# Merge gates of attentions 2 and 3 as seven products of quarters, with sums of tokens made on the chip

## The chip, the cores and the metric

The kernel runs on one core of a Trainium2 chip. The metric is the time on the device of one execution, in microseconds (us). Three runs of the kernel before took 1600.72, 1601.18 and 1605.92 us. One further execution was taken with the profiler. TensorE (PE in the rows) does matrix products, VectorE (DVE), ScalarE (ACT) and GpSimd (POOL) work on elements, SyncE (SP) issues most transfers.

## The reference

An encoder of two layers, 512 tokens of width 1024. In each layer four attentions of different kinds read projections of the normalised input `h`, and their outputs are merged:

```
h = rmsnorm(x);  p = h @ w_in[l]                 # 13824 columns: q, k, v, gate, merge
merged = 0
for n, o in enumerate((oa, ob, oc, od)):         # four attention outputs, 512 wide
    gated = o * silu(p.gate[n])                  # 512 columns
    y = gated @ w_branch[l, n]                   # 512 -> 1024
    merged += sigmoid(p.merge[n]) * y            # 1024 columns
x = x + merged @ w_out[l]                        # 1024 -> 1024
```

The product that the change touches is `p.merge[n] = h @ w_in[l][:, merge n]`, 512 x 1024 by 1024 x 1024, for n = 2 and 3.

## The kernel before

All matrix products run in float16 with operands split into a high and a low half: each product of two values takes three matmuls (high by high, low by high, high by low). `hT_h` and `hT_l` hold the halves of `h`, features on the partitions, 512 tokens along the row.

Weights come from HBM in pieces of 1 MB as float32, in the order of the table `ORDER`. `dma_w` issues the two loads of a piece, `load_w` converts each half piece (128 x 1024) on ACT into `whi` and on DVE into the remainder `wlo`, and `take_w` hands a piece out and starts the next: conversion runs two pieces ahead, loading three. Staging tiles `wst` have five buffers.

`merge(n)` goes feature tile by feature tile (8 of 128 features): `proj_t` makes the gate's 128 x 512 from 8 slices of `h` with 24 matmuls of 512 columns, ACT makes the sigmoid in three passes (Exp, Ln, Exp), `proj_t` makes the branch's 128 x 512 with 12 matmuls, and DVE multiplies the two and adds them to `acc`. The four merges are spread: `weave` runs the steps of an attention with steps of other work between them, and merge(0), (1), (2) are such filling for attentions B, C and D0; merge(3) runs alone behind D0.

`output` makes `merged @ w_out` in seven products of quarters in place of eight (a Winograd form of Strassen's scheme). Operands are cut in halves along both sides, the seven products run on quarters and on sums of quarters, and the results are combined by adding in PSUM and on DVE. The weights' sums are made while loading: a tile `wsum` takes a quarter by an ordinary load, and POOL issues DMAs that add another quarter to it (`accum_op`). One running sum serves four of the seven products: the first use, then three adds, each of which must wait until the sum before has been converted. The token side's sums (`xs`, two kinds for each of four row groups, in `forms`) are made on DVE and ACT, three of the four while merge(3) still runs. In the program's count the products are named by their form, in the order 1, 2, 5, 6, 7, 3, 4; 1, 2 and 4 read a quarter as it is, 5, 6, 7 and 3 read `xs`.

Each engine runs its instructions in its own order, fixed when the program is built: a scheduler with a model of the times reorders the instructions within what dependences allow.

## Time and profile before

| | |
|---|---|
| median of three runs | 1601.18 us |
| profiled execution | 1608.34 us, of which the span from the first to the last instruction is 1606.6 us |
| granted TensorE clock, mean | 0.997 of full |
| busy TensorE / DVE / ACT / POOL | 1588.5 / 1109.9 / 975.7 / 61.0 us |

An engine's busy time is the time in which at least one of its instructions runs; weight loads of TensorE are counted apart (PEld). Matmuls overlap in the rows (a matmul of 512 columns lasts 0.38 us and the next starts 0.22 us later), so the distance between two starts is what one costs. On DVE and ACT too a row's duration holds an overlap of some 0.1 us with its neighbours.

### The profile page before, as it was taken

How to read it: one execution, taken by the hardware profiler on the slowest of the kernel's cores; microseconds unless marked ns; L12 is line 12 of the kernel's file. 1: busy time of each engine (PE TensorE's matmuls, PEld its weight loads, DVE VectorE, ACT ScalarE, POOL GpSimd, SP SyncE). 2: the span in 40 equal slices, each digit the busy share in tenths (PEclk: the TensorE clock that was granted, in tenths of full speed). 3: DMA queues.
4: the chain of work that ended last, by engine and by line, in shares of the span. 5: the costliest groups of instructions: out<-in, count | busy, mean ns of one | idle time of the engine just before them, and what ended most of it. 6: DMA issues, size and time to landing. Idle time of an engine off the chain costs nothing.

```text
span 1606.6 us, 26657 instructions
## 1 busy us (share of the span) xinstructions
PE 1588.5 (99%) x10222; PEld 834.0 (52%) x10222; DVE 1109.9 (69%) x2188; ACT 975.7 (61%) x1799; POOL 61.0 (4%) x145
## 2 busy tenths in 40 slices
PE   8899999999999999999999999999999999999998
PEld 3555455644555554554455545556455655445444
DVE  7599667854757675775877876687556675658565
ACT  7387755765746464654567766566666465556452
POOL 4000000000000000120000000000000000001000
PEclk9999999999999999999999999999999999999999
DMA  9758333522556666465455672335334675743644
GB/s 295 183 150 159 114 97 105 139 79 86 138 139 168 152 196 161 124 188 131 122 189 142 141 156 91 97 97 120 118 99 112 157 184 130 207 131 108 176 92 105
DMA packets 223729, 224.18 MB, mean 140 GB/s; under 512 B 167080, under 2 KB 179384, under 8 KB 223600
## 3 DMA queue, kind: packets, MB, share of 16 engines
q1 hardware_dynamic: 220000, 209.37, 49.1%
q0 software_dynamic: 3600, 13.10, 4.0%
q8 instruction: 80, 1.31, 0.3%
q14 instruction: 49, 0.40, 0.1%
HBM read 172.33 MB, written 10.24 MB: 114 GB/s over the span
## 4 chain that ended last, share of the span: by engine, by line
PE 89%; DMA 3%; DVE 3%; issue 3%; POOL 1%; ACT 1%; POOLq 0%; DVEq 0%; ACTq 0%
PE mm L475 15%; PE mm L473 15%; PE mm L474 15%; PE mm L491 10%; PE mm L492 10%; PE mm L493 10%; PE s L647 3%; PE s L648 3%; PE pv L653 2%; PE pv L654 2%; PE pv L652 2%; DVE wlo L180 1%; DMA wsum<-in_wf_dram 1%; DMA gb<-in_qk_gain_dram 1%; DMA rope_t<-in_rope_dram 0%
## 5 line engine op out<-in xcount | busy, mean ns | idle before, releaser
L473 PE MATMUL mm<-whi,hT_h 128*128 128x512 f16 (+1 forms) x1280 | 473.4, 370 | 8.5 <-DVE qn L543 3.0
L475 PE MATMUL mm<-whi,hT_l 128*128 128x512 f16 (+1 forms) x1280 | 473.5, 370 | 0.6 <-DVE hT_l L289 0.6
L474 PE MATMUL mm<-wlo,hT_h 128*128 128x512 f16 (+1 forms) x1280 | 473.3, 370 | 0.3 <-DVE wlo L180 0.3
L180 DVE SCALAR_TENSOR_TENSOR wlo<-wst,whi 128x1024 f16<-128x1024 f32 (+1 forms) x256 | 300.3, 1206 | 116.8 <-ACT whi L179 116.2
L179 ACT ACTIVATE whi<-wst 128x1024 f16<-128x1024 f32 (+1 forms) x256 | 252.4, 1034 | 134.0 <-PE mm L492 112.1
L473 PEld LDWEIGHTS <-hT_h 128*128 128x128 f16 x1280 | 131.8, 103 | 132.5 <-DVE v L583 4.1
L475 PEld LDWEIGHTS <-hT_l 128*128 128x128 f16 x1280 | 131.7, 103 | 130.9 <-DVE hT_l L289 1.5
L474 PEld LDWEIGHTS <-hT_h 128*128 128x128 f16 x1280 | 131.8, 103 | 130.3 <-issue 6.6
L493 PE MATMUL mm<-hT_h,wlo 128*128 128x512 f16 x512 | 194.0, 379 | 0.0
L492 PE MATMUL mm<-hT_l,whi 128*128 128x512 f16 x512 | 194.0, 379 | 0.0
L491 PE MATMUL mm<-hT_h,whi 128*128 128x512 f16 x512 | 194.0, 379 | 0.0
L638 ACT ACTIVATE t<-t,nm 128x512 f32<-128x512 f32 (+2 forms) x224 | 131.6, 601 | 90.2 <-DVE t L802 36.2
L643 DVE TENSOR_TENSOR pl<-t,ph 128x512 f16<-128x512 f32 (+2 forms) x224 | 118.1, 543 | 32.0 <-ACT ph L642 31.0
L493 PEld LDWEIGHTS <-wlo 128*128 128x128 f16 x768 | 75.1, 98 | 88.1
L491 PEld LDWEIGHTS <-whi 128*128 128x128 f16 x768 | 75.1, 98 | 86.3
L492 PEld LDWEIGHTS <-whi 128*128 128x128 f16 x768 | 75.1, 98 | 85.7
L653 PE MATMUL pv<-v,ph 128*128 128x64 f16 (+1 forms) x960 | 118.7, 201 | 0.0
L652 PE MATMUL pv<-v,ph 128*128 128x65 f16 (+1 forms) x960 | 118.6, 200 | 0.0
L654 PE MATMUL pv<-v,pl 128*128 128x65 f16 (+1 forms) x960 | 116.9, 199 | 0.0
L642 ACT ACTIVATE ph<-t 128x512 f16<-128x512 f32 (+2 forms) x224 | 109.7, 505 | 2.4 <-PE pv L654 0.7
L500 ACT ACTIVATE sq<-mm 128x512 f32<-128x512 f32 (+1 forms) x96 | 51.8, 540 | 83.8 <-PE mm L475 82.5
L648 PE MATMUL s<-qs,kk 128*128 128x512 f16 (+4 forms) x384 | 100.5, 292 | 0.0
(213 smaller groups left out, 2279.9 us busy)
## 6 DMA issues: line engine op xcount, KB each, us to landing
wst<-in_wf_dram SPq DMA_DIRECT2D x260, 512.0 KB
wsum<-in_wf_dram POOLq DMA_DIRECT2D x12, 512.0 KB, 6.7
dsc<-num SPq DMA_DIRECT2D x16, 260.0 KB
xt<-in_x_dram SPq DMA_DIRECT2D x8, 512.0 KB
bias_b<-lines SPq DMA_DIRECT2D x8, 448.0 KB
bias_a<-lines SPq DMA_DIRECT2D x16, 192.0 KB
num<-dsc SPq DMA_DIRECT2D x8, 260.0 KB
n<-dsc SPq DMA_DIRECT2D x8, 260.0 KB
```

Of the source, the lines that this page charges most:

```text
L179: S.activation(hi[:, a], st[:, e:e + step], AF.Copy if sc is SW else AF.Identity, scale=sc)
L180: V.scalar_tensor_tensor(lo[:, a], st[:, e:e + step], sc, hi[:, a], op0=ALUm, op1=ALUs)
L473: PE.matmul(p[:, :ncol], a, wh, start=(k == 0), stop=False)
L474: PE.matmul(p[:, :ncol], a, wl, start=False, stop=False)
L475: PE.matmul(p[:, :ncol], b, wh, start=False, stop=(k == 7))
L491: PE.matmul(p, wh[:, k, f], rh[:, k], start=(k == 0), stop=False)
L492: PE.matmul(p, wh[:, k, f], rl[:, k], start=False, stop=False)
L493: PE.matmul(p, wl[:, k, f], rh[:, k], start=False, stop=(k == nk - 1))
L648: PE.matmul(p, klo, q, start=False, stop=True)
L652: PE.matmul(o, ph, vt[:, 0:d + 1], start=start, stop=False)
L653: PE.matmul(o[:, 0:d], ph, vt[:, d + 2:2 * d + 2], start=False, stop=False)
L654: PE.matmul(o, pl, vt[:, 0:d + 1], start=False, stop=stop)
```

## The change

The gate products of merges 2 and 3 also take the seven-product form, now with features on the output's partitions: the weight quarter is the loaded operand and 256 tokens stream. merge(1) takes the place of merge(2) beside attention D0, and attention C keeps 16 steps of filling in place of 24. Merges 2 and 3 both run alone behind D0. The sums of tokens for them (`hx`) are made from float32 sums of `hT_h` and `hT_l` that POOL adds up (`h_sums`, tiles `hf`). The sums for the output (`xs`) are now all made inside `output`. Several tiles share other buffers: the running sum of weights those of the bias tables (`bias`), `xs` those of the probabilities, the norm's gain those of `kk2`, the gated values of attention 3 those of `qx`.

```diff
 ORDER = (
...
-    + _gate(2) + _merge(1) + _qd(1) + _kvd(1)
+    + _gate(2) + _qd(1) + _kvd(1)
     + _qd(2) + _kvd(2)
-    + _qd(0) + _gate(3) + _kvd(0) + _merge(2)
-    + _merge(3) + _rows("out", 0, 512) + _rows("out", 512, 512)
+    + _qd(0) + _gate(3) + _kvd(0) + _merge(1)
+    + _square("in", MERGE0 + 2048, 2) + _square("in", MERGE0 + 3072, 3) + _square("out", 0)
 )
...
-                st = chain_t[j] = at.tile([128, 1024], F32, tag="ph", name="wsum")
+                st = chain_t[j] = at.tile([128, 1024], F32, tag="bias", name="wsum")
...
-        t = at.tile([128, D], F32, tag="bias", name="gain_b")
+        t = qk.tile([128, D], F32, tag="kk2", name="gain_b")
...
+    def sums(m, j, f, g, t, dst, scale):
+
         a, c, b, d = f[:, 0:256], f[:, 256:512], g[:, 0:256], g[:, 256:512]
...
+        if m == 0:
+            V.tensor_tensor(t[0][:, 0, :], d, c, op=ALUs)
+            V.tensor_tensor(t[0][:, 1, :], a, c, op=ALUs)
+        else:
+            V.scalar_tensor_tensor(t[1][:, 0, :], a, -1.0, t[0][:, 0, :], op0=ALUm, op1=ALUs)
+            V.scalar_tensor_tensor(t[1][:, 1, :], t[1][:, 0, :], -1.0, b, op0=ALUm, op1=ALUs)
+        hi, lo = dst[m, 0][:, :, j, :], dst[m, 1][:, :, j, :]
+        S.activation(hi, t[m], AF.Copy, scale=scale)
+        V.scalar_tensor_tensor(lo, t[m], scale, hi, op0=ALUm, op1=ALUs)
...
+    def h_sums():
...
+        for j in range(4):
+            fg = []
+            for k in (j, j + 4):
+                r = at.tile([128, 512], F32, tag="t", name="hf", bufs=3)
+                G.tensor_tensor(r, hT_h[:, k, :], hT_l[:, k, :], op=ALUa)
+                fg.append(r)
+            t = [tmp.tile([128, 2, 256], F32, tag="o", name="xf") for _ in range(2)]
+            for m in range(2):
+                sums(m, j, fg[0], fg[1], t, hx, 1.0)
...
+    def merge_s(n):
...
+        def product(p, w, xh, xl, i, start):
+
+            for q in range(2):
+                c = slice(256 * i + 128 * q, 256 * i + 128 * q + 128)
+                joint = q == 1 or not start
+                for k in range(4):
+                    PE.matmul(p[:, q, :], w[0][:, k, c], xh[:, k, :], start=start and q == 0 and k == 0, stop=False,
+                              skip_group_check=joint)
+                    PE.matmul(p[:, q, :], w[0][:, k, c], xl[:, k, :], start=False, stop=False, skip_group_check=joint)
+                    PE.matmul(p[:, q, :], w[1][:, k, c], xh[:, k, :], start=False, stop=k == 3, skip_group_check=joint)
...
+        form(1, pa, True)
+        r1 = copies(pa, tmp, "qn")
+        form(2, pb, True)
         for i in range(2):
...
+            V.tensor_tensor(r1[i], pb[i], r1[i], op=ALUa)
+            gate(r1[i], r1[i], 1.0)
+        wb = take_w(("br", n), 0)[0]
+        for i in range(2):
+            gain(branch(wb, i, 0), r1[i], 0, i, 0)
+        y21 = copies([branch(wb, i, 256) for i in range(2)], at, "t", bufs=3)
+        form(5, pc, True)
...
+        form(4, pa, False)
+        for i in range(2):
+            e = tmp.tile([128, 2, 256], F32, tag="sig", name="e")
+            gate(pa[i], e, 1.0)
+            gain(y21[i], e, 0, i, 256)
...
+        natural(range(8), slice(0, 256))
...
+        for j0 in (0, 2):
+            for m in range(2):
+                for j in (j0, j0 + 1):
+                    sums(m, j, acc[:, j, :], acc[:, j + 4, :], ts[j % 2], xs, SM)
+        natural(range(4, 8), slice(256, 512))
...
         weave(attn_c(l, r["qC"], *r["kC"], r["vC"]),
-              chain(gates(2), merge(1), proj_q(r, l, "D1", 3584, True), proj_k(r, l, "D1", 5120, True),
-                    proj_v(r, "D1", 6656, 8, HD, True)), 24)
+              chain(gates(2), proj_q(r, l, "D1", 3584, True), proj_k(r, l, "D1", 5120, True),
+                    proj_v(r, "D1", 6656, 8, HD, True)), 16)
...
-        weave(attn_d0(l, r["qD0"], *r["kD0"], r["vD0"]), merge(2), 8)
+        weave(attn_d0(l, r["qD0"], *r["kD0"], r["vD0"]), merge(1), 8)
...
-        for ft, _ in enumerate(merge(3)):
-            if ft >= 4:
-                forms(ft - 4)
+        h_sums()
+        merge_s(2)
+        merge_s(3)
```

How this moves instructions is shown at three places. The first is TensorE inside the merge behind D0. Before, at the end of merge(3) in layer 0 (`mm` is a PSUM tile, `gT` the gated values):

```order
L491 LDWEIGHTS whi
L491 MATMUL mm<-gT,whi 128x512
L492 LDWEIGHTS whi
L492 MATMUL mm<-gT,whi 128x512
L493 LDWEIGHTS wlo
L493 MATMUL mm<-gT,wlo 128x512
```

After, at the start of the first product of merge(2) in layer 0 (`pa` is one of its PSUM tiles):

```order
L1020 LDWEIGHTS whi
L1020 MATMUL pa<-hT_h,whi 128x256
L1022 LDWEIGHTS whi
L1022 MATMUL pa<-hT_l,whi 128x256
L1023 LDWEIGHTS wlo
L1023 MATMUL pa<-hT_h,wlo 128x256
```

Each matmul keeps its own weight load and streams half as many columns.

The second place is POOL in layer 0, from D0 to the output stage. Before (`gk`, `cosq` and so on are the next layer's tables, and the only adds, `wst` and `wsum`, are those of the output):

```order
L438 DMA gb<-in_qk_gain_dram 128x512
L440 DMA rope_t<-in_rope_dram 128x512
L443 TENSOR_TENSOR gk<-gb 128x256
L448 TENSOR_TENSOR cosq<-rope_t,gb 128x256
L450 TENSOR_TENSOR sinq<-rope_t,gb 128x4x32 x2
L448 TENSOR_TENSOR cosk<-rope_t,gb 128x256
L450 TENSOR_TENSOR sink<-rope_t,gb 128x4x32 x2
L587 MEMSET v 128x16
L158 DMA wst<-in_wf_dram 128x1024 x2
L158 DMA wsum<-in_wf_dram 128x1024 x6
```

After, the part at the start of merge(2) and in merge(3) (`hf` are the sums of the two halves of `h`):

```order
L1004 TENSOR_TENSOR hf<-hT_h,hT_l 128x512 x3
L171 DMA wsum<-in_wf_dram 128x1024
L600 MEMSET v 128x16
L171 DMA wsum<-in_wf_dram 128x1024 x2
L1004 TENSOR_TENSOR hf<-hT_h,hT_l 128x512 x2
L171 DMA wsum<-in_wf_dram 128x1024 x2
L1004 TENSOR_TENSOR hf<-hT_h,hT_l 128x512 x3
L171 DMA wst<-in_wf_dram 128x1024
L171 DMA wsum<-in_wf_dram 128x1024 x2
L171 DMA wst<-in_wf_dram 128x1024
L171 DMA wsum<-in_wf_dram 128x1024 x4
```

The eight sums of `h` stand between the adds of the running sum of weights; the tables of the next layer have moved behind the adds of merge(3).

The third place is DVE in layer 0 where the sums for the output are made. Before (`xf` is a sum of quarters, `xs` its low half, `hT_l` now the low half of the merged values):

```order
L946 TENSOR_TENSOR acc<-acc,sig 128x512
L960 TENSOR_TENSOR xf<-acc 128x256
L962 SCALAR_TENSOR_TENSOR xf<-acc,xf 128x256
L963 SCALAR_TENSOR_TENSOR xf<-xf,acc 128x256
L967 SCALAR_TENSOR_TENSOR xs<-xf,xs 128x2x256
L961 TENSOR_TENSOR xf<-acc 128x256
L967 SCALAR_TENSOR_TENSOR xs<-xf,xs 128x2x256
L945 SCALAR_TENSOR_TENSOR sig<-mm,sig 128x512
L946 TENSOR_TENSOR acc<-acc,sig 128x512
```

After, in the output stage (`xt` is the residual that takes the products' results):

```order
L193 SCALAR_TENSOR_TENSOR wlo<-wst,whi 128x1024
L1128 SCALAR_TENSOR_TENSOR xt<-pb,xt 128x512
L982 SCALAR_TENSOR_TENSOR xs<-xf,xs 128x2x256
L1128 SCALAR_TENSOR_TENSOR xt<-pb,xt 128x512
L193 SCALAR_TENSOR_TENSOR wlo<-wst,whi 128x1024
L975 TENSOR_TENSOR xf<-acc 128x256
L976 TENSOR_TENSOR xf<-acc 128x256
L975 TENSOR_TENSOR xf<-acc 128x256
L976 TENSOR_TENSOR xf<-acc 128x256
L193 SCALAR_TENSOR_TENSOR wlo<-wst,whi 128x1024
L982 SCALAR_TENSOR_TENSOR xs<-xf,xs 128x2x256
L978 SCALAR_TENSOR_TENSOR xf<-acc,xf 128x256
```

A row group's sums stood between two feature tiles of merge(3); now they stand among the weight conversions and results of the output stage.

## Rows read from the trace of the kernel before

**Rows 1.** The page, busy us (share of the span) and instructions of each engine.
```profile
PE 1588.5 (99%) x10222; PEld 834.0 (52%) x10222; DVE 1109.9 (69%) x2188; ACT 975.7 (61%) x1799; POOL 61.0 (4%) x145
```

**Rows 2.** Waits of TensorE: for whom, us in total, times, longest; first and last.
```profile
PE mm L473 <- DVE qn L543: 3.0, 1, 3.0
...
PE pa L994 <- DVE xt L1000: 0.2, 1, 0.2
```

**Rows 3.** Windows: length, busy us by engine, granted clock, DMA share, GB/s.
```profile
773.80:810.00 36.20, 36.03 (x170) 16.52 (x169) 30.64 (x39) 20.91 (x31) 3.46 (x4) 1.00 0.66 175
800.00:840.00 40.00, 38.05 (x188) 19.01 (x187) 29.92 (x46) 24.14 (x55) 0.00 (x0) 0.96 0.55 182
880.00:960.00 80.00, 80.00 (x568) 41.14 (x565) 68.66 (x159) 53.55 (x109) 0.13 (x1) 1.00 0.72 155
```

**Rows 4.** TensorE in order of time, merge(3) of layer 0: start, us, what.
```profile
744.86 0.38 PE L491 MATMUL mm<-hT_h,whi 128*128 128x512 f16 x1
...
773.78 0.38 PE L493 MATMUL mm<-gT,wlo 128*128 128x512 f16 x1
```

**Rows 5.** TensorE in order of time, the 256-column projection of layer 1.
```profile
838.97 0.27 PE L473 MATMUL mm<-whi,hT_h 128*128 128x256 f16 x1
...
844.10 0.27 PE L475 MATMUL mm<-whi,hT_l 128*128 128x256 f16 x1
```

**Rows 6.** TensorE in order of time, values of D0 in layer 1.
```profile
1445.46 0.19 PE L652 MATMUL pv<-v,ph 128*128 128x65 f16 x1
...
1446.28 0.19 PE L652 MATMUL pv<-v,ph 128*128 128x65 f16 x1
```

**Rows 7.** DVE in order of time, around the start of layer 0's output stage.
```profile
767.84 0.42 DVE L975 SCALAR_TENSOR_TENSOR hT_l<-acc,hT_h 128x256 f16<-128x256 f32 x1
768.17 0.42 DVE L960 TENSOR_TENSOR xf<-acc 128x256 f32<-128x256 f32 x1
...
769.85 0.68 DVE L967 SCALAR_TENSOR_TENSOR xs<-xf,xs 128x512 f16<-128x512 f32 x1
770.45 1.02 DVE L975 SCALAR_TENSOR_TENSOR hT_l<-acc,hT_h 128x256 f16<-128x256 f32 x2
...
773.53 2.35 DVE L180 SCALAR_TENSOR_TENSOR wlo<-wsum,whi 128x1024 f16<-128x1024 f32 x2
775.80 0.68 DVE L945 SCALAR_TENSOR_TENSOR sig<-mm,sig 128x512 f32<-128x512 f32 x1
```

**Rows 8.** ACT by line and form: count, busy us, mean ns; idle before it.
```profile
L179 ACT ACTIVATE whi<-wst 128x1024 f16<-128x1024 f32 x248 | 247.8, 1047 | 131.8 <-PE mm L492 112.1 <-PE mm L475 19.1 <-PE pa L996 0.2
...
L939 ACT ACTIVATE sig<-sig,one 128x512 f32<-128x512 f32 x64 | 46.0, 719 | 1.4
...
L938 ACT ACTIVATE sig<-mm 128x512 f32<-128x512 f32 x64 | 37.5, 586 | 35.1 <-PE mm L493 34.8
```

**Rows 9.** The running sum of weights: its DMAs, issue to landing.
```profile
DMA to landing us min/median/max: 5.3/6.7/9.9
```

**Rows 10.** DVE in order of time, while POOL makes rotation tables.
```profile
709.43 2.94 DVE L180 SCALAR_TENSOR_TENSOR wlo<-wst,whi 128x1024 f16<-128x1024 f32 x2 [4.03 <-ACT whi L179]
...
712.83 1.62 DVE L180 SCALAR_TENSOR_TENSOR wlo<-wst,whi 128x1024 f16<-128x1024 f32 x1
```

**Rows 11.** POOL in order of time, the same stretch.
```profile
709.16 0.72 POOL L448 TENSOR_TENSOR cosq<-rope_t,gb 128x256 f32<-128x256 f32 x1 [5.73 <-DMA rope_t<-in_rope_dram]
709.85 2.83 POOL L450 TENSOR_TENSOR sinq<-rope_t,gb 128x128 f32<-128x128 f32 x2
```

**Rows 12.** TensorE in order of time, at the start of layer 1.
```profile
813.84 0.38 PE L475 MATMUL mm<-whi,hT_l 128*128 128x512 f16 x1
815.76 0.39 PE L473 MATMUL mm<-whi,hT_h 128*128 128x512 f16 x1 [1.53 <-ACT hT_h L288]
...
818.43 0.63 PE L473 MATMUL mm<-whi,hT_h 128*128 128x512 f16 x1
818.86 0.63 PE L474 MATMUL mm<-wlo,hT_h 128*128 128x512 f16 x1
```

More of the change, by code (lines that the diff above doesn't have):

```diff
@@ L133, in encoder @@
     w_tiles = {}
-    pieces = [(l, c, l * len(ORDER) + j) for l in range(L) for c, j in _forms(ORDER)]
+    pieces = [(l, c, l * len(PACKED) + j) for l in range(L) for c, j in TAKEN]
     w_stage, chain_t = {}, {}
@@ L144, in packed @@
             return wf[(at_ + q) * PIECE:(at_ + q + 1) * PIECE].rearrange("(p n) -> p n", p=128)[:, e:e + 1024]
-        load, add = FORM[c[1]] if c[0] == "out" else (0, None)
+        load, add = FORM[c[1]] if c[0] == "form" else (0, None)
         w_stage[i] = []
@@ L150, in dma_w @@
                 st = chain_t[j]
[L151 to L152 removed]
+            elif c[0] == "form" and c[1] == 0:
+                st = chain_t[j] = at.tile([128, 1024], F32, tag="bias", name="wsum")
             else:
@@ L1017, in output @@
                 (4, pa, False, 0, 2, 1.0))):
-            w = take_w("out", n)[0]
+            w = take_w("form", n)[0]
             for i in range(2):
```

133 lines of the change are left out of this document (93 added, 40 removed).

## The prediction

> **What bounds the kernel now.** I read the busy shares first, then who TensorE waits for, then TensorE's rows in order of time. TensorE (PE) is marked busy for 1588.5 us of the 1606.6 us span, VectorE (DVE) for 69%, ScalarE (ACT) for 61% [rows 1]. Matmul ends are modelled, so the share alone proves little. The waits settle it: twelve groups, from 3.0 us down to 0.2 us [rows 2]. Matmuls also start at an even pace where the change works: 135 matmuls of 512 columns from 744.86 to 773.78 us, so 134 steps of 0.2158 us [rows 4]. So the kernel lasts as long as TensorE takes to issue its matmuls, and a matmul less is worth its step, as long as nothing new makes TensorE wait.
>
> **What goes.** A merge of old has 8 feature tiles of 24 gate and 12 branch matmuls, 288 of 512 columns: 288 x 0.2158 = 62.2 us. The seven-product form has 7 x 48 gate and 8 x 24 branch matmuls, 528 of 256 columns. Their step stands in the projection of 256 columns: 48 matmuls from 838.97 to 844.10 us, 47 steps of 0.1091 us [rows 5]. That gives 57.6 us. Two merges in each of two layers: 4 x 4.5 = 18.1 us less. Were 256 columns to cost a tenth more than this, 5.8 us a merge would go and nothing be won; 48 even steps speak against that.
>
> Twice as many weight loads come with it. A value matmul of 65 or 64 columns, each with a load of its own, steps at 0.0304 us (27 steps from 1445.46 to 1446.28 us [rows 6]; as many loads as matmuls in rows 1), so the load hides behind far less than 256 columns. The Trainium skill ("TensorE: Matmul & The Clock Gate", section "LDWEIGHTS (loading the stationary operand)") gives a load of 128 columns as 128 / 1.2, about 107 ns, and under "The mechanism" says that it overlaps matmuls only where the row groups differ. By that, 960 more loads would add some 100 us by estimate; the trace does not agree, since load and matmul together took 30 ns in those rows.
>
> **What is added beside TensorE.** Each such merge converts 18 half pieces of weights where it converted 12: 6 x 1.05 us on ACT [rows 8], 6 x 1.13 us on DVE [rows 7]. A merge then holds 18 x 1.05 + 24 gate passes x 0.64 + 8 copies x 0.6 = 39 us of ACT [rows 8], and 18 x 1.13 + 22 x 0.60 = 34 us of DVE, with 10 us more for the token sums in merge(2). All of it lies beside 57.6 us of TensorE, so on average it costs nothing; the chains below do. Eight POOL adds of 512 KB a merge are new; one lands in 6.7 us (5.3 to 9.9) [rows 9].
>
> **Term 1, the output stage of each layer.** Before, three of the four sums for the output were formed while merge(3) still ran, and in the window 773.8 to 810 us TensorE is busy for 36.03 of 36.20 us although DVE already has 30.64 us of work there [rows 3]. Now all four need the quarter that form 4 writes last. Three sums at four short and two long operations (4 x 0.33 + 2 x 0.60 = 2.5 us each [rows 7]) move into the stage: 30.6 + 7.6 = 38 us of DVE in 36.2 us. In the new order of DVE, from the gain that follows form 4 to the last operand of product 5, stand 14 operations of 512 columns, 16 of 256 and 6 of 1024: 14 x 0.60 + 16 x 0.33 + 6 x 1.13 = 20.5 us [rows 7]. The gain can start 0.7 us before the stage (form 4's first half is 2.6 us old by then, less three passes of ACT at 0.59 to 0.72 us [rows 8]), so the operand is there 19.8 us into it. TensorE has 82 matmuls ahead of it, 17.7 us. So 2.1 us are lost at least. DVE also stands for the third weight sum (added 6.7 us after the second is converted, about 1 us before the stage), some 1 to 2 us, and product 6 takes its last operands 3 us later still. I take 4 us a layer, bounds 2 and 6: +8 us.
>
> **Term 2, the start of merge(2) in each layer.** The running sum of weights now lies in the bias buffers, and its second half can't load before D0's last bias is read. From that score to the first product TensorE has 50 matmuls of 512 columns and 60 value matmuls, 12.6 us, so the load lands some 6.7 us ahead of the product (0.6 us for DVE's bias add, and 5.3 for the load, the low end of rows 9). Then come the conversion of the first sum (2.2 us), the add to the second (6.7), its conversion (2.2), the add to the third (6.7), ACT's half of that (1.0), and behind it on ACT's queue the gate, 4.1 us with two conversions in it, and DVE's gain, 0.6: 23.5 us, or 16.8 us into the merge. The third branch product needs that gain to free its bank, and TensorE reaches it after 164 matmuls, 17.9 us. There are 1.1 us to spare, less an issue of about 1 us for each add. The token sums meet the same adds: in POOL's order two of the eight `hf` sums stand behind the adds to the third sum and three behind those to the fourth, and DVE's sums wait for each.
>
> POOL and DVE also get in each other's way. When POOL made the rotation tables, two weight conversions took 2.94 us and a third 1.62 us, where two take 2.35 [rows 7, 10]; POOL's two operations of 128 columns took 2.83 us beside 0.72 us for one of 256 [rows 11]. That is the rule of the Trainium skill ("SBUF — State Buffer", section "Who interferes with whom"): a VectorE instruction with two inputs in SBUF and a GpSimd instruction that reads SBUF lock each other out for a whole instruction. The trace agrees as to direction, the delays being part of an instruction. A sum of 128 x 512 on POOL I take as twice the 0.72 us, 1.4 us. Three of them fall into DVE's dense run, up to 4 us more on it. Without the meeting, term 2 is 0; with it and two adds at the slow end (9.9 instead of 6.7) it is 10. I take 2.5 us a layer, near the median row: +5 us.
>
> **Term 3, the clock.** After a wait at 813.84 us (1.92 us to the next start) 512 columns took 0.43 us a step, that is 1.2 of 2.4 GHz [rows 12]; the granted clock of that window of 40 us is 0.96 [rows 3], so 1.6 us of it were lost. The new waits are of that length. I put one such fall in the program, +1.5 us; bounds 0 and 6, one for each of the four places.
>
> **Priced at nothing.** Attention C loses the 8 tiles of merge(1), and keeps 16 steps of projections. Attention A of layer 1 runs with 16 as well, and TensorE is busy there for 80.00 of 80.00 us [rows 3]; what it costs if that cover fails is a rival below. D0 gets merge(1) for merge(2), the same instructions. The next layer's rotation tables go from D0 to the output stage on POOL, ahead of the last add: two landings at 6.7 us [rows 9] and six operations at 0.7 to 1.4 us [rows 11] behind the third sum's adds put it some 21 us into the stage, and its product comes at 31; later than that, TensorE waits for the rest. On SP, x's second half waits for the buffer of merge(3)'s gated values, last read before form 4, and is needed after product 5, some 15 us later; the two weight loads behind it have a product to spare. The norm gain's new buffer was last read in attention C.
>
> **Sum.** -18.1 + 8 + 5 + 1.5 = -3.6 us. Against the profiled execution (1608.34 us, span 1606.6) that is 1604.7; the median of the runs, 7.2 us lower, becomes 1597.6 us. What a measurement of this kernel can tell from no change is 0.3%, 4.8 us, so the forecast lies just inside "the same".
>
> **Rivals.**
> *The waits are hidden* (30%). POOL's add lands early enough and the clock holds; only the output stage pays, 3 us a layer: -18.1 + 6 = -12.1, 1589 us. For it: the 1.1 us to spare in term 2, and TensorE's order there already puts other products into the gap. Against: the lock in rows 10 and 11.
> *The weight sums bind* (17%), slower. Place: from the last bias of D0 to the third branch product. Each us that the two adds take beyond the median and 1.1 us is a us of TensorE, in both layers. At 9.9 us each: 2 x (6.4 - 1.1 + 2 of lock) = 14.6; with 6 us a layer in the output stage and two falls of the clock, 14.6 + 12 + 3 - 18.1 = +11.5, 1613 us. The kernel is slower from 18.1 us of new waits on. For it: two adds in a row on one chain, which the old stage had only with several products between. Against: the median row.
> *Attention C runs dry* (6%): a head's eight ACT passes (8 x 0.65 us, by rows 8) lie open once a layer, 10 us on top of the forecast, 1608 us. For it only that its fill falls by a third; against it rows 3.
> *The loads show* (3%). 4 x 240 = 960 matmuls more, each with a load: if even the 0.0304 us of rows 6 stood in the open for each, 29 us come on top of the forecast, 1627 us. Nothing speaks for it in rows 5 and 6. It is what the page's rule on overlap would do, with another price.
>
> **How the numbers follow.** Forecast 44%, alone 1593 to 1603 us. Faster by over 0.3% (below 1596.4): the hidden case but for a part, 0.28, and a fifth of the forecast's, 0.09: 0.37. Slower by over 0.3% (above 1606): two thirds of the binding case, 0.11, and most of the last two, 0.07: 0.18. The same: 0.45. The range goes from the hidden case with 2.5 us a layer, 1588, to within the binding one, 1609.
>
> **What would show it.** Right: steps of 0.109 us in both merges; TensorE waiting for DVE's `xs` in the output stage, 2 to 6 us a layer, and for `hx` or the banks of `y` early in merge(2). Wrong: no such waits (then 1585 to 1590), a step above 0.12 us, or waits for `wlo` of the running sum over 5 us a layer.

## The result: slower by 1.3%

The changed kernel takes 1624.01 us (median of 4 runs, 1622.59 to 1626.43); the kernel before, on the same chips, 1602.63 us (4 runs, 1600.72 to 1605.92). The ratio is 1.0131, 95% interval 1.0119 to 1.0143. Forecast were 1597.6 us and a range of 1588 to 1609. The profiled execution after took 1623.0 us (span 1621.2); that of before, 1608.34 us, lay above its own median, so the two profiles differ by less (14.6 us of span) than the medians (21.4 us).

The page of the changed kernel: the engines [rows 1], the queue in which POOL's transfers run (packets, MB, share of 16 DMA engines), the chain of waits by engine, and POOL's adds (KB each, us to landing).

```profile
PE 1580.0 (97%) x11182; PEld 929.6 (57%) x11182; DVE 1177.0 (73%) x2292; ACT 1022.8 (63%) x1879; POOL 111.9 (7%) x193
...
q0 software_dynamic: 8208, 29.88, 9.9%
...
PE 80%; DMA 8%; DVE 5%; issue 4%; ACT 2%; POOL 1%; SPq 0%; POOLq 0%; DVEq 0%
...
wsum<-in_wf_dram POOLq DMA_DIRECT2D x36, 512.0 KB, 6.0
```

The same queue and chain on the page of before:

```profile
q0 software_dynamic: 3600, 13.10, 4.0%
...
PE 89%; DMA 3%; DVE 3%; issue 3%; POOL 1%; ACT 1%; POOLq 0%; DVEq 0%; ACTq 0%
```

The waits of TensorE after [rows 2]; the longest group of before was 3.0 us:

```profile
PE pa L1124 <- DVE xs L982: 7.0, 4, 3.4
PE y L1020 <- DVE r_qn L1046: 5.6, 4, 2.5
PE pa L1020 <- ACT hx L981: 3.3, 2, 1.7
...
PE pc L1124 <- DVE xs L982: 2.0, 3, 1.3
```

Windows of the changed kernel [rows 3]: the start of merge(2) in layer 0, its output stage, the boundary to layer 1, the start of merge(2) in layer 1.

```profile
662.00:672.00 10.00, 5.69 (x38) 4.09 (x36) 10.00 (x15) 5.82 (x9) 3.26 (x4) 0.84 0.86 201
...
781.00:798.00 17.00, 10.90 (x41) 3.66 (x40) 16.83 (x28) 8.88 (x14) 6.51 (x7) 0.90 0.67 170
...
812.00:828.00 16.00, 12.51 (x52) 6.24 (x51) 13.65 (x20) 9.04 (x23) 0.00 (x0) 0.79 0.79 293
...
1463.00:1473.00 10.00, 3.87 (x25) 2.52 (x23) 9.89 (x13) 8.14 (x12) 4.12 (x4) 0.73 0.77 145
```

TensorE is idle for 3.5 to 6.1 us in each, and the granted clock falls with it. Before, it was full in merge(3) and all but full in the output stage of layer 0 [rows 3, 4]; at the boundary of the layers it already stood for 1.95 us of a window of 40 [rows 3]. Between the waits its pace is as forecast [rows 5]: 67 steps of 256 columns from 654.76 to 662.08 us are 0.1093 us each. Then it stands. TensorE in order of time, layer 0, from product 2 to the third branch product:

```profile
654.76 0.27 PE L1022 MATMUL pb<-hT_l,whi 128*128 128x256 f16 x1
...
662.08 0.27 PE L1023 MATMUL y<-gT,wlo 128*128 128x256 f16 x1
...
664.04 0.27 PE L1023 MATMUL pa<-hx,wlo 128*128 128x256 f16 x1
666.01 0.38 PE L1020 MATMUL pa<-hx,whi 128*128 128x256 f16 x2 [1.69 <-ACT hx L981]
...
669.16 0.37 PE L1020 MATMUL y<-gT,whi 128*128 128x256 f16 x1 [2.45 <-DVE r_qn L1046]
```

ACT in the same stretch converts the sum for product 5 from 648.55 us. The next add of the chain, for product 6, can only go out behind that, and ACT stands 4.45 us for the first half of it and 0.85 us for the second, with a copy of `pa` and the gate behind them in its order:

```profile
648.55 1.99 ACT L192 ACTIVATE whi<-wsum 128x1024 f16<-128x1024 f32 x2
...
656.74 1.06 ACT L192 ACTIVATE whi<-wsum 128x1024 f16<-128x1024 f32 x1 [4.45 <-DMA wsum<-in_wf_dram]
657.71 0.58 ACT L1052 ACTIVATE r_qn<-pa 128x512 f32<-128x512 f32 x1
...
659.65 1.06 ACT L192 ACTIVATE whi<-wsum 128x1024 f16<-128x1024 f32 x1 [0.85 <-DMA wsum<-in_wf_dram]
```

The gate ends at 664.9 us. DVE then has two conversions ahead of the gain that frees the bank for the third branch product:

```profile
664.86 3.31 DVE L193 SCALAR_TENSOR_TENSOR wlo<-wst,whi 128x1024 f16<-128x1024 f32 x2
...
668.43 0.68 DVE L1046 SCALAR_TENSOR_TENSOR r_qn<-y,r_qn 128x512 f32<-128x512 f32 x1
```

POOL has two more `hf` sums (the first of them below) behind adds that wait for a landing and a conversion:

```profile
659.56 0.89 POOL L171 DMA_DIRECT2D wsum<-in_wf_dram  x1 [1.89 <-DMA wsum<-in_wf_dram]
662.26 0.87 POOL L171 DMA_DIRECT2D wsum<-in_wf_dram  x1 [1.81 <-DVE wlo L193]
662.82 1.49 POOL L1004 TENSOR_TENSOR hf<-hT_h,hT_l 128x512 f32<-128x512 f16 x1
```

To place the loss I took, over each trace, the distance of every matmul's start to the next, less the usual step of its shape (0.216 us for 512 columns, 0.109 for 256). The usual steps sum to 1577.3 us before and 1558.7 after: 18.6 us less. What is over (waits and steps at the lower clock) went from 23.8 to 57.1 us:

| us over the usual steps | before | after |
|---|---|---|
| start of merge(2), layers 0 and 1 | 0 | 6.3 + 9.9 |
| start and later part of merge(3), both | 0 | 2.0 + 2.5 |
| output stage, both | under 0.4 | 8.6 + 5.8 |
| boundary of the layers | 4.1 | 7.1 |
| first 60 us of the program | 17.1 | 13.9 |
| rest | 2.6 | 1.0 |

### The profile page after: what moved, and what is told of

Same layout as the page of the kernel before. It is cut to its first block, busy times and chain, and to the rows that moved or that the text cites. A ratio compares the mean times of both kernels' runs of the same rounds, so it can differ in the third digit from the quotient of the medians.

```text
span 1621.2 us, 28895 instructions
## 1 busy us (share of the span) xinstructions
PE 1580.0 (97%) x11182; PEld 929.6 (57%) x11182; DVE 1177.0 (73%) x2292; ACT 1022.8 (63%) x1879; POOL 111.9 (7%) x193
## 3 DMA queue, kind: packets, MB, share of 16 engines
q1 hardware_dynamic: 220000, 209.37, 48.6%
## 4 chain that ended last, share of the span: by engine, by line
PE 80%; DMA 8%; DVE 5%; issue 4%; ACT 2%; POOL 1%; SPq 0%; POOLq 0%; DVEq 0%
PE mm L486 16%; PE mm L488 16%; PE mm L487 16%; DMA wsum<-in_wf_dram 5%; PE mm L506 5%; PE mm L504 5%; PE mm L505 5%; PE s L660 3%; PE s L661 3%; DVE wlo L193 2%; PE pv L666 2%; PE pv L667 2%; PE pv L665 2%; ACT whi L192 1%; PE y L1020 1%
## 5 line engine op out<-in xcount | busy, mean ns | idle before, releaser
L193 DVE SCALAR_TENSOR_TENSOR wlo<-wst,whi 128x1024 f16<-128x1024 f32 (+1 forms) x248 | 292.0, 1210 | 78.1 <-ACT whi L192 77.6
L192 ACT ACTIVATE whi<-wst 128x1024 f16<-128x1024 f32 (+1 forms) x248 | 244.6, 1033 | 82.5 <-PE mm L505 39.6
L661 PE MATMUL s<-qs,kk 128*128 128x512 f16 (+4 forms) x384 | 100.0, 292 | 0.0
L660 PE MATMUL s<-qs,kk 128*128 128x512 f16 (+4 forms) x384 | 99.0, 292 | 0.8 <-DMA kk<-st 0.8
L193 DVE SCALAR_TENSOR_TENSOR wlo<-wsum,whi 128x1024 f16<-128x1024 f32 x48 | 57.9, 1225 | 54.5 <-ACT whi L192 53.9
L506 PE MATMUL mm<-hT_h,wlo 128*128 128x512 f16 x256 | 97.0, 379 | 0.0
L504 PE MATMUL mm<-hT_h,whi 128*128 128x512 f16 x256 | 97.0, 379 | 0.0
L505 PE MATMUL mm<-hT_l,whi 128*128 128x512 f16 x256 | 97.0, 379 | 0.0
L665 PEld LDWEIGHTS <-ph 128*128 128x128 f16 x960 | 89.7, 96 | 10.3
```

The costliest lines, as they stand in the source:

```text
L192: S.activation(hi[:, a], st[:, e:e + step], AF.Copy if sc is SW else AF.Identity, scale=sc)
L193: V.scalar_tensor_tensor(lo[:, a], st[:, e:e + step], sc, hi[:, a], op0=ALUm, op1=ALUs)
L504: PE.matmul(p, wh[:, k, f], rh[:, k], start=(k == 0), stop=False)
L505: PE.matmul(p, wh[:, k, f], rl[:, k], start=False, stop=False)
L506: PE.matmul(p, wl[:, k, f], rh[:, k], start=False, stop=(k == nk - 1))
L661: PE.matmul(p, klo, q, start=False, stop=True)
```

## The experiments

Times are medians; ratios, with 95% intervals, are to the kernel before, run on the same chip.

**The change in parts: what can be left out.** Without the token sums of `h`:

```diff
-        h_sums()
...
-            xh, xl = part(f, (hT_h, hT_l), hx)
+            xh, xl = part({5: 1, 7: 1, 6: 2, 3: 2}.get(f, f), (hT_h, hT_l), hx)
```

> Left out: the sums of tokens of h (hx); the four products of merges 2 and 3 that read them read a quarter of h as it is, and POOL's, DVE's and ACT's work for them is gone. The adds to the weights stay. Theory A (TensorE waits at the start of merge(2) because DVE's and POOL's queues hold the token sums): the waits and half-clock steps there go, 6.3 us in layer 0 and 9.9 in layer 1 of the changed kernel's trace, so about 1608 us. Theory B (the running weight sum with its adds one behind the other binds there): the products and gains still come late, at most 4 us less, 1620 us or more.

1618.86 us, ratio 1.0092 (1.0068 to 1.0116): 5 us less, nearer to B. By the steps above the start of merge(2) did fall from 16.2 to 6.7 us, but waits came up elsewhere (merge(3) of layer 1: 6.1 us).

Without the token sums of the output:

```diff
-                    sums(m, j, acc[:, j, :], acc[:, j + 4, :], ts[j % 2], xs, SM)
...
-            xh, xl = (v[:, :, t] for v in part(f, (mh, ml), xs))
+            xh, xl = (v[:, :, t] for v in part({5: 1, 7: 1, 6: 2, 3: 2}.get(f, f), (mh, ml), {}))
```

> Left out: the sums of tokens for the output (xs); all seven products of the output read quarters as they are. Theory A (in the output DVE has more work before product 5's operand than TensorE has products): the waits and half-clock steps of the output go, 8.6 us in layer 0 and 5.8 us in layer 1, so about 1610 us, and perhaps 3 us more at the layer's boundary if that only follows from DVE's backlog. Theory B (the weights' running sum is late in the output): TensorE still waits there, 3 us a layer or more, for wlo of the third and fourth sum; 1617 us or more.

1621.53 us, 1.0102 (1.0068 to 1.0135); the runs spread from 1615.88 to 1625.73. B holds. In the output stage of layer 0 one wait of 7.4 us took the place of those for `xs`. TensorE's row among the waits of that stretch:

```profile
PE pa L1113 <- DVE xt L1119: 7.4, 1, 7.4
```

ACT there, and DVE, whose order has the remainder `wlo` of a late sum before the `xt` that frees the bank:

```profile
798.73 1.06 ACT L192 ACTIVATE whi<-wsum 128x1024 f16<-128x1024 f32 x1 [4.85 <-DMA wsum<-in_wf_dram]
802.48 1.06 ACT L192 ACTIVATE whi<-wsum 128x1024 f16<-128x1024 f32 x1 [2.70 <-DMA wsum<-in_wf_dram]
```

```profile
803.57 1.23 DVE L193 SCALAR_TENSOR_TENSOR wlo<-wsum,whi 128x1024 f16<-128x1024 f32 x1 [2.53 <-ACT whi L192]
804.72 1.28 DVE L1119 SCALAR_TENSOR_TENSOR xt<-pa,xt 128x512 f32<-128x512 f32 x2
```

Without the sums of weights:

```diff
-            if load is None:
-                st = chain_t[j]
...
+            st = wp.tile([128, 1024], F32, tag="wst", name="wst", bufs=WST)
+            dma = nc.sync.dma_start(out=st, in_=packed(add if load is None else load, e))
```

> Left out: the sums of weights. Every product loads one quarter by an ordinary load from SP into the rotating staging buffers; POOL issues no adds. Theory A (DVE alone is behind): little changes, since DVE has the same instructions: 1619 to 1624 us. Theory B (the adds bind, by their chain or by holding the sums hf behind them on POOL's queue): the 16 us of waits at the start of merge(2) go and some of the output's, 1600 to 1608 us.

1601.41 us, 0.9985 (0.9972 to 0.9997): 22.6 us less than the changed kernel, B. This run leaves out all 48 adds, the 16 that the kernel before has too among them, and loads the first quarter of each square into staging like any other piece.

The order alone, on the kernel before:

```diff
-    + _gate(2) + _merge(1) + _qd(1) + _kvd(1)
+    + _gate(2) + _qd(1) + _kvd(1)
...
-    + _qd(0) + _gate(3) + _kvd(0) + _merge(2)
-    + _merge(3) + _rows("out", 0, 512) + _rows("out", 512, 512)
+    + _qd(0) + _gate(3) + _kvd(0) + _merge(1)
+    + _merge(2) + _merge(3) + _rows("out", 0, 512) + _rows("out", 512, 512)
...
+        run(merge(2))
         for ft, _ in enumerate(merge(3)):
```

> The kernel before with only the order of the merges changed: merge(1) beside D0 in place of merge(2), 16 in place of 24 steps beside attention C, merges 2 and 3 alone behind D0 in their old form, the output's sums as before. Theory A (the loss is all in the new stages): 1601 to 1604 us, as before. Theory C (the new neighbours cost too: attention C or D0 runs dry): 1607 us or more, with waits of TensorE beside C or D0.

1603.84 us, 0.9996 (0.9982 to 1.0010): it costs nothing, A.

**What about the adds is dear.** The place of the running sum, and plain loads in the adds' place:

```diff
-                st = chain_t[j] = at.tile([128, 1024], F32, tag="bias", name="wsum")
+                st = chain_t[j] = (at if j else qk).tile([128, 1024], F32, tag=("kk2", "bias")[j], name="wsum")
```

> The changed kernel with another place for the weights' running sum: its first half in the buffer kk2, which nothing uses during D0, its second half in the first bias buffer that comes free; the norm's gain goes to a bias buffer. Theory B1 (the chain of adds starts too late, because the second half of the sum loads only when D0's last bias is read): the waits at the start of merge(2), 16 us in the two layers, mostly go: 1607 to 1613 us. Theory B2 (the chain is too slow wherever it starts, two adds behind each other and ACT standing for each): at most 5 us less, 1619 to 1624 us.

1627.99 us, 1.0149 (1.0133 to 1.0164); the interval overlaps with that of the changed kernel, and nothing is gained. But this does not decide between B1 and B2, as only the first link came early. The second half of the first sum is converted from 612.00 us, where it was 641.08. The sum for product 5 stands in ACT's order behind the weights of the branch, which wait for a matmul of merge(1):

```profile
646.14 2.00 ACT L192 ACTIVATE whi<-wst 128x1024 f16<-128x1024 f32 x2 [0.32 <-PE mm L505]
...
649.29 1.99 ACT L192 ACTIVATE whi<-wsum 128x1024 f16<-128x1024 f32 x2
```

The first product starts at 649.64 us here, and the first half of the sum for product 6 is converted 9.6 us behind it, against 10.3 us in the changed kernel. What a chain that is earlier in all its links would give, no run shows.

```diff
-                dma = nc.gpsimd.dma_start(out=st, in_=packed(add, e), accum_op=ALUa)
+                dma = nc.gpsimd.dma_start(out=st, in_=packed(add, e))
```

> Every add of POOL's becomes a plain load by POOL into the same tile, with the same waits and the same bytes (the sums of weights are left out). Theory B3 (the adding itself is dear: the transfer that reads and writes the tile takes long, and loads the DMA engines): the time falls to 1603 to 1611 us. Theory B2 (the order is what costs: convert, issue, land, convert): landing falls little below 5.9 us and the time stays at 1617 to 1624 us.

1605.74 us, 1.0017 (1.0008 to 1.0027): 18.3 us less with the same waits, issues and bytes. B3. Both the landing and the load on the DMA engines fall, so this run does not part the two. The page of this run has the same packets and MB as after, and little over half of their share:

```profile
q0 software_dynamic: 8208, 29.88, 5.8%
...
wsum<-in_wf_dram POOLq DMA_DIRECT2D x36, 512.0 KB, 4.7
```

What ACT stands for transfers into the running sum's tile, in us in total, times and longest: after, then this run, then before.

```profile
ACT whi L192 <- DMA wsum<-in_wf_dram: 46.2, 20, 6.9
```

```profile
ACT whi L192 <- DMA wsum<-in_wf_dram: 27.4, 17, 4.1
```

```profile
ACT whi L179 <- DMA wsum<-in_wf_dram: 12.2, 4, 4.3
```

By ACT's rows one by one, 19.0 of the 46.2 us are for the ordinary load of the first quarter. The other 27.2 us, 12 times, are for adds, and all 12 are for the two halves of the sum for product 6, whose add follows directly on the conversion of the sum before. With plain loads these are 14.2 us, 9 times.

The time over the usual steps, as in the table of the result, shows where it goes (us, both layers together):

| | changed | plain loads for adds | no adds | no adds, no `hx` (a later run) |
|---|---|---|---|---|
| start of merge(2) | 16.2 | 6.4 | 5.4 | 0 |
| merge(3) | 4.5 | 0.9 | 0 | 0 |
| output stage | 14.4 | 12.8 | 13.2 | 14.4 |
| boundary of the layers | 7.1 | 4.1 | 1.6 | 1.4 |

So half of what the adds cost lies at the start of merge(2), and almost nothing in the output stage.

Without adds the queue holds 0.9% of a span of 1599.3 us, 14.4 us of all 16 engines. So the 48 adds take 0.099 x 1621.2 - 14.4 = 146 us, 3.0 us each, and plain loads in their place 0.058 x 1603.2 - 14.4 = 79 us, 1.6 each: 1.86 times. The Trainium skill ("Collectives: The Full Stack", section "The bandwidth ceiling: the fold count and why AG ≠ RS ≠ AR") says that adding in a transfer itself is not what slows, but the two reads that each piece needs. That is told of transfers between cores; the factor of 1.86 here is of that size, but the page of the profile counts the same packets and MB in both runs, so no run here shows a second read.

More adds in shorter chains:

```diff
-FORM = ((0, None), (1, None), (None, 2), (None, 3), (2, 3), (3, None), (None, 1))
+FORM = ((0,), (1,), (0, 2), (0, 2, 3), (2, 3), (3,), (None, 1))
```

> The running sum no longer goes through products 1, 5, 6: product 5 loads a quarter into staging and adds one, product 6 loads one into the running tile and adds two, product 4 adds to that; 10 POOL adds in place of 8 and 11 in place of 10 MB... of loads a square. Theory B2 (the chain of convert and add binds): the waits at the start of merge(2) fall from 16 to under 6 us, and the output's by some: 1605 to 1612 us. Rival B4 (POOL's queue or the DMA engines' load binds, whoever waits): no gain, 1620 us or more.

1652.67 us, 1.0300 (1.0251 to 1.0349): B4, and by far. It is a heavier load than was expected: 11 MB a square in place of 8 (branch weights not counted), and 60 adds in place of 48. Landing of both kinds on its page:

```profile
wsum<-in_wf_dram POOLq DMA_DIRECT2D x36, 512.0 KB, 8.5
...
wst<-in_wf_dram POOLq DMA_DIRECT2D x24, 512.0 KB, 12.0
```

Adds that nobody waits for:

```diff
+                    chain_t["dead"] = qk.tile([128, 2, 1024], F32, tag="v", name="dead")
...
-                dma = nc.gpsimd.dma_start(out=st, in_=packed(add, e), accum_op=ALUa)
+                dma = nc.gpsimd.dma_start(out=chain_t["dead"][:, j, :], in_=packed(add, e), accum_op=ALUa)
```

> The adds are issued by POOL as before, with the same bytes in the same queue, but into a tile that nothing reads; the products that need a sum of weights convert the unsummed quarter (the sums of weights are left out). So the DMA engines keep the adds' load and no engine waits for one. Theory B5 (ACT, whose order is fixed, stands for the landing of sums, 46 us in the changed kernel, and what lies behind it there comes late): 1600 to 1607 us, as with no adds at all. Theory B4 (the adds take so much of the DMA engines, 40% of them at the start of merge(2), that all other loads come late): 1615 us or more.

1634.22 us, 1.0189 (1.0174 to 1.0204). This does not separate the two: each add waits on POOL for the one before to land, and the `hf` sums stand behind them. From the waits of 640 to 690 us:

```profile
POOL dead L175 <- DMA dead<-in_wf_dram: 22.6, 8, 5.7
...
DVE xf L979 <- POOL hf L1008: 12.5, 3, 6.0
```

So again without `hf` (the edit above and that of the first run), and beside it neither adds nor `hf` (that of the first run and that of the run without sums of weights):

> Adds into a tile that nothing reads, as in the run before, and without the sums of h's tokens, so that nothing of merge(2) stands behind the adds on POOL (both kinds of sums are left out for merges 2 and 3; the output's token sums stay). Theory B5 (what costs is that conversions, and what stands behind them on ACT, wait for an add to land): no engine waits for an add any more, so 1595 to 1604 us, as with no adds or below. Theory B4 (the adds' load on the DMA engines delays the ordinary loads): as much as with the adds in use and no token sums, 1618.9 us, give or take 4.

> No adds (every product loads one quarter as it is) and no sums of h's tokens. Next to the run with dead adds (1611.9 us) it differs by the adds' load alone. Theory B4 (that load delays others): 1595 to 1602 us, so 10 us or more for the load. Theory B5 (only waiting for a landing costs): 1608 to 1612 us.

1611.87 us (1.0051, 1.0037 to 1.0065) with dead adds, 1596.50 us (0.9950, 0.9936 to 0.9964) without. Adds in use, without `hf`, had taken 1618.86. So of 22.4 us that the adds cost there, 7.0 go when nobody reads their results, and 15.4 stay: the second run falls to B4, the first between the two theories. The windows of the two runs (DMA share is the number before the last):

```profile
646.00:700.00 54.00, 51.84 (x485) 46.18 (x482) 28.61 (x37) 30.47 (x43) 13.11 (x14) 1.00 0.98 222
```

```profile
646.00:700.00 54.00, 54.00 (x508) 48.44 (x504) 33.42 (x44) 33.19 (x45) 0.17 (x1) 1.00 0.58 175
```

The 15.4 us are not the load alone, as the two runs differ in a second thing. With dead adds the first quarter of a square still goes into the running tile, which comes free late, and ACT stands for that ordinary load (27.2 us in all, by its waits); without adds it is loaded ahead into staging, and ACT stands 2.4 us for loads of weights in all. What the run with dead adds loses more over the usual steps lies at the ends of merge(2) and merge(3), where ACT stands so. In layer 0, at the end of merge(2):

```profile
690.63 1.06 ACT L196 ACTIVATE whi<-wsum 128x1024 f16<-128x1024 f32 x1 [4.88 <-DMA wsum<-in_wf_dram]
```

That load was issued at 680.19 us and took 10.4 us. In the changed kernel the same load, issued at 686.64 us, was there 5.1 us later. So the adds' load does delay other loads when it is dense, and dead adds are denser: they run as fast as they land, 13 in that stretch, while the changed kernel's window 646.4 to 662 us has a share of 0.91, that of 672 to 770 us 0.72. How the 22 us divide between waiting for an add and its load on the DMA engines is not shown.

**Attempts on the order and the sums.** The last quarter in another role, so that three of the output's four sums need not wait for it (halves of tokens and features exchanged in merges 2 and 3):

```diff
+            half, tok = 1 - half, 256 - tok
             ac = acc[:, 4 * half + 2 * i:4 * half + 2 * i + 2, tok:tok + 256]
...
+        if n == 3:
+            output_sums()
         form(4, pa, False)
```

> The halves of features and of tokens change places in merges 2 and 3, so that the quarter that comes last is the one which only one of the output's four sums needs; the other three sums, and products 5 and 7's operands, are made before the last product of merge(3) ends. Theory A (in the output TensorE waits for sums of tokens that all need the last quarter): the output's waits fall from 8.6 and 5.8 us to 3 or less each, and the layer's boundary gives 2 us back: 1612 to 1616 us. Theory B (the weights' sum is late there too): 1619 us or more.

1628.28 us, 1.0151 (1.0135 to 1.0168): theory B. The waits for `xs` went and one for the last quarter came, product 2's operand on ACT, which stood for the next sum of weights. TensorE's row among the waits, and ACT:

```profile
PE pb L1143 <- ACT hT_h L1107: 7.0, 1, 7.0
```

```profile
776.62 1.06 ACT L193 ACTIVATE whi<-wsum 128x1024 f16<-128x1024 f32 x1 [2.98 <-DMA wsum<-in_wf_dram]
...
780.22 1.99 ACT L193 ACTIVATE whi<-wst 128x1024 f16<-128x1024 f32 x2
782.11 1.32 ACT L1107 ACTIVATE hT_h<-acc 128x256 f16<-128x256 f32 x4
```

The token sums before merge(2):

```diff
+        m1 = merge(1)
-        weave(attn_d0(l, r["qD0"], *r["kD0"], r["vD0"]), merge(1), 8)
+        weave(attn_d0(l, r["qD0"], *r["kD0"], r["vD0"]), itertools.islice(m1, 6), 6)
         h_sums()
+        run(m1)
```

> D0 gets six of merge(1)'s eight tiles; the sums of h's tokens are made beside the other two tiles, 15 us of TensorE, before merge(2) begins. Theory A (the token sums in the same queues as the chain cost, 5 us by the run that left them out): 1615 to 1620 us. Rival C (D0 runs dry with six tiles, or the chain of weights binds whatever else is moved): 1622 us or more.

1629.64 us, 1.0157 (1.0141 to 1.0173): rival C, by its second half. The token sums are out of the way, and in layer 0 the gated gain still starts 22.4 us after the first product, as in the changed kernel (22.0). TensorE waits 17.8 us for it in the two layers, and ACT stands 44.8 us for transfers into the running tile, where it was 46.2.

```profile
PE y L1021 <- DVE r_qn L1047: 17.8, 4, 6.2
```

The second sum's conversion held behind the gate's last pass (`g1`), in two tries:

```diff
+        if src == "form" and pieces[i][1][1] == 2 and late:
+            holds = ((late.pop(),),) * 2
...
+                if a < 2 or not chained(i + a):
...
-            dma_w(i + AHEAD)
+            for a in (AHEAD - 1, AHEAD):
+                if all(k in w_tiles for k in range(i, i + a) if chained(k)) or not chained(i + a):
+                    dma_w(i + a)
...
+        late.append(g1)
```

> The changed kernel, but in merges 2 and 3 the conversion of the second weight sum is held on ACT and DVE until the gate of the first quarter has been issued, so that ACT no longer stands for the add with the gate behind it. Same adds, same work. Theory B5: the waits at the start of merge(2), 16 us with the half-clock steps, fall to 8 or less: 1610 to 1617 us. Rival B2 (the chain itself is too long, and its later start only delays product 6): 1622 us or more.

1725.07 us, 1.0749 (1.0721 to 1.0777). It tells nothing of the question: the edit loads pieces a second time that are converted already, 345.70 MB in the queue of ordinary loads in place of 209.37.

```diff
-                if all(k in w_tiles for k in range(i, i + a) if chained(k)) or not chained(i + a):
+                if i + a not in w_tiles and (not chained(i + a) or all(k in w_tiles for k in range(i, i + a) if chained(k))):
```

> The hold of the second sum's conversion behind the first quarter's gate, in merges 2 and 3, now without loading any piece twice. Theory B5: ACT does the gate before it stands for the add; the waits at the start of merge(2), 16 us with the half-clock steps, fall to 8 or less: 1610 to 1617 us. Rival B2 (the chain then ends later still, and product 6 waits for it): 1622 us or more.

1622.50 us, 1.0116 (1.0102 to 1.0130): by its range B2, 1.5 us below the changed kernel in intervals that overlap. The start of merge(2) lost some 18 us over the usual steps, not less than the 16.2 us of the changed kernel. It is no clean test of ACT's order: the edit also converts every running sum, the output's too, one piece ahead in place of two.

POOL's additions as instructions:

```diff
-                dma = nc.gpsimd.dma_start(out=st, in_=packed(add, e), accum_op=ALUa)
+                more = wp.tile([128, 1024], F32, tag="wst", name="wst", bufs=WST)
+                dma = nc.sync.dma_start(out=more, in_=packed(add, e))
+                G.tensor_tensor(st, st, more, op=ALUa)
```

> No accumulating transfers: the quarter to be added is loaded by SP into staging, and POOL adds it with an instruction of 128 x 1024 (estimate 2.4 to 3 us each, from 1.15 to 1.3 us for the hf sums of 128 x 512). Theory B3 (the accumulating transfer is what is dear): near the plain loads' 1605.7 us, 1603 to 1612. Rival (POOL's 48 additions hold up DVE, about 1 us each as beside the hf sums, and need staging buffers that the loads then lack): 1618 us or more.

1664.09 us, 1.0379 (1.0363 to 1.0394), the rival; which of its two parts weighs more is not shown. An addition takes 2.7 us, and POOL waits 57.4 us for conversions on DVE and 42.8 us for loads into the five staging buffers that now feed both (line, count, busy, mean ns, idle before):

```profile
L173 POOL TENSOR_TENSOR wsum<-wsum,wst 128x1024 f32<-128x1024 f32 x36 | 97.9, 2726 | 113.4 <-DVE wlo L195 57.4 <-DMA wst<-in_wf_dram 42.8 <-ACT r_t L1054 3.8
```

**Does the form pay anywhere?** One merge in the new form between the halves of an old one, then the same with DVE adding the merge's weights:

```diff
-        merge_s(2)
-        merge_s(3)
+        m3 = merge(3)
+        run(itertools.islice(m3, 4))
+        merge_s(2)
+        for j, _ in enumerate(m3):
+            forms(j)
```

> A version that keeps the seven-product form for merge(2) alone and puts it between the two halves of merge(3) in its old form: merge(1) beside D0, four tiles of merge(3), merge(2), four tiles of merge(3), output with three of its four sums made beside merge(3) as before. If the waits come from the neighbours (the sums of h and the first adds at the start, the late quarter at the output) and not from the form, 2 x 4.65 us go and 1 to 3 us of waits a merge stay: 1596 to 1600 us, faster than before by 0.2 to 0.5%. If the adds bind wherever the form stands, 6 us or more of waits a merge: 1605 us or more.

1619.12 us, 1.0103 (1.0085 to 1.0121), with a wide spread (1613.89 to 1624.15; the profile is of the fastest). The adds bind here too: ACT, and what TensorE waited for most,

```profile
693.40 1.06 ACT L193 ACTIVATE whi<-wsum 128x1024 f16<-128x1024 f32 x1 [7.16 <-DMA wsum<-in_wf_dram]
694.36 0.61 ACT L1041 ACTIVATE r_qn<-r_qn 128x512 f32<-128x512 f32 x1
```

```profile
PE pa L1125 <- DVE xt L1131: 6.7, 2, 4.7
PE y L1021 <- DVE r_qn L1047: 6.6, 2, 3.8
```

```diff
+                if at_ % len(PACKED) < len(PACKED) - 4:
+                    more = wp.tile([128, 1024], F32, tag="wst", name="wst", bufs=WST)
+                    dma = nc.sync.dma_start(out=more, in_=packed(add, e))
+                    V.tensor_tensor(st, st, more, op=ALUa)
+                else:
+                    dma = nc.gpsimd.dma_start(out=st, in_=packed(add, e), accum_op=ALUa)
```

> The version with merge(2) alone in the new form, between the halves of merge(3); its weights' sums are now added by DVE from quarters that SP loads (8 additions of 128 x 1024 a merge, 1.2 us each by DVE's other operations of that size), and only the output keeps POOL's accumulating transfers. If those transfers and their landing are what the form pays for: 1595 to 1600 us, faster than before by 0.2 to 0.5%. If DVE's 10 us a merge more, or the extra staging buffers, cost as much as the adds did: 1608 us or more.

1607.09 us, 1.0014 (1.0004 to 1.0025), between what the two theories gave: 12 us less than with POOL's adds, but no better than before. TensorE's waits for the gated gain are gone; those for the output remain:

```profile
PE pa L1130 <- DVE xt L1136: 6.2, 2, 4.3
```

**The floor.** No sums of any kind (the edits of the first three runs together):

> No adds, no sums of h's tokens, no sums of tokens for the output: the matmuls of the changed kernel in their order, and nothing that makes operands beyond quarters. If the three kinds of sums are all that costs, the 18.6 us of the shorter matmul stream are there in full: 1584 to 1590 us, and against the run without adds and hx the output's sums are worth 8 to 14 us. If something else costs (the new order of buffers, the gate's chain, the clock): 1594 us or more.

1582.86 us, 0.9868 (0.9854 to 0.9881), a little under what was expected; granted clock 0.998. So without the three kinds of sums the loss is gone. This is a floor and no kernel: it also lacks the adds and the output's sums that the kernel before makes, so not all of the difference is the price of the change. Built up from here: the output's `xs` 13.6 us (1596.50), `hx` 4.9 (1601.41), the adds 22.6 (1624.01). TensorE's waits without adds and `hx`, the only large group:

```profile
PE pa L1116 <- DVE xs L974: 8.1, 2, 4.4
```

The parts depend on each other: with the adds in, leaving out `xs` gives 2.5 us and not 13.6, as an add is next in line.

No version was found that beats the kernel before.

## Why the prediction was wrong, step by step

**What goes** was right: 18.1 us forecast, 18.6 in the steps. The floor's 1582.86 us is 20 us below the median of before, but it also lacks sums that the kernel before makes. The weight loads stayed hidden; that rival is out.

**Priced at nothing**: the order, right (1603.84 us).

**What is added beside TensorE** is the step that failed, and with it term 2. It said of "Eight POOL adds of 512 KB a merge" that one lands in 6.7 us, "beside 57.6 us of TensorE"; the adds got a price at the start of merge(2), some allowance in the output stage, and none elsewhere. The landing was right (6.0 us). Measured, all adds cost 22.6 us, of which 18.3 go when the same transfers do not add. By the steps 10.8 us of this lie at the start of merge(2), 4.5 in merge(3), 5.5 at the boundary of the layers and 1.2 in the output stage. The adds' time on the DMA engines was not counted at all: 32 new adds, each 3.0 us of all 16, in merges whose loads rise from 6 to 10 MB. It could have been read from the page of before: 4.0% of 1606.6 us is 64 us, less the 14.4 that other transfers in that queue take, for 16 adds: 3.1 us each. Whether it is this time or the wait for the landing that costs, the runs do not part.

**Term 2, the start of merge(2)**: 2.5 us a layer forecast, 0 to 10; 6.3 and 9.9 measured, clock included. The chain was named rightly, add behind conversion, the gate behind both on ACT, the third branch product behind the gain. In layer 0 its first links came out as worked: the sum for product 5 is converted from 2.1 us after the first product and the first half of the sum for product 6 from 10.3 us; the working has 2.2 and 11.1. Then it was sized too small. The second half of that sum is converted from 13.2 us, the gate ends at 18.4 us (worked: 16.2), and the gain, behind the two conversions of 3.31 us on DVE, ends at 22.6 us (worked: 16.8); by the working TensorE is at its bank after 17.9 us. The token sums share the loss: without `hx` 6.7 us of the 16.2 stay, without adds 5.4, without both nothing. The place was right; 2.5 us a layer, set near the median landing, left too little for the second half, for DVE's order and for the clock.

**Term 1, the output stage**: 4 us a layer forecast, 2 to 6; 8.6 and 5.8 measured. Without adds and `hx` the wait for `xs` is 8.1 us in the two layers. That this equals the forecast is in part luck, since the forecast held 1 to 2 us a layer for the third weight sum, which that run leaves out. The steps at the lower clock behind the wait are 2.9 us a layer more, and the two together, 13.9 us, are what `xs` costs (13.6 in time). The mechanism was right, the clock was missing.

**Term 3, the clock**: 1.5 us forecast, 0 to 6. The mean granted clock was 0.992 of 1621.2 us, so 13.0 us lost, and 0.997 of 1606.6 before, 4.8 us: 8 us. The fall after a wait, known from [rows 12], came in each of the four windows shown above (0.73 to 0.90), not in one place of the program. One such term for every new wait would have come near.

**The boundary of the layers**, not forecast: 3 us more, between the late last additions and the transposes of the next layer (window 812 to 828 us, clock 0.79).

**The rivals.** "The weight sums bind" was the nearest in kind and too small, 1613 us: it put them between D0's last bias and the third branch product alone. Its reason, that the old stage had two adds in a row "only with several products between", is a misreading: the old output took the seven products in the same order, and ACT stood 12.2 us for four adds there while TensorE lost under 0.4 us. "The waits are hidden" took the adds for hidden, and the forecast nearly so. The sign to watch for that rival, waits of TensorE for `wlo`, did not come: it waits for `y`, `hx` and `xs`, that is for what stands behind `wlo` and `whi` in other engines' order.

What stays open: how much of the adds' price is the wait for their landing and how much their load on the DMA engines; and what a chain with all its links earlier would give.

## What to carry to other kernels

Price a new transfer twice, by its landing at each place where an engine stands for it and by the time that it takes of the DMA engines, which the queue's share on the page gives, before asking what it hides behind. A wait for a transfer in the fixed order of an engine is paid by what stands behind it there, so TensorE's waits name another operand than the one that is late. When a shorter stream of matmuls needs operands made of sums, find its floor first, without the sums: here it lay 20 us under the kernel before, and three kinds of sums took 41 us.

## What was not expected of the hardware

An accumulating transfer of 512 KB took 3.0 us of the 16 DMA engines where a plain one by the same queue took 1.6, landed in 6.0 in place of 4.7 us, and held POOL 0.86 in place of 0.53 us for its issue (medians of the rows of `wsum`). An addition of two 128 x 1024 float32 tiles took 2.73 us on POOL and 1.22 us on DVE.
